# Three gate products moved from beside the chunked scan to between the convolution's tiles

## The chip, the cores and the metric

The kernel runs on one core of one Trainium2 chip. The metric is the device time of one execution in microseconds (us). Three runs of the kernel before gave 1928.44, 1927.75 and 1927.33 us; the median is 1927.75.

Short names: TensorE is PE (matrix products), VectorE is DVE (elementwise), ScalarE is ACT (elementwise, and copies out of PSUM), GpSimd is POOL, SyncE is SP (it issues most DMAs). Each runs its own instructions in order.

## What is computed

One encoder layer on 512 tokens of width 1024, in float32:

```
proj = rmsnorm(x) @ w_in                  -> u_s5, z, xbc, dt_raw, gate_a, gate_b
y_a  = glu(gelu(s5_bidirectional(u_s5)))               # the state-space branch (S5)
xbc  = silu(conv5(xbc) + b)  -> xs (8 tiles), B (2), C (2)
y_b  = ssd_bidirectional(z, xs, B, C, dt) @ w_out      # the chunked scan (SSD)
h    = x + (sigmoid(gate_a)*y_a + sigmoid(gate_b)*y_b) @ w_o
h    = h + peer_ffn(rmsnorm(h));  out = rmsnorm(h)
```

A tile is 128 of the output columns of a projection, for all 512 tokens. `gate_b` has eight tiles (gb0 to gb7), and so have `z`, `gate_a` and the convolution's `xs` (x0 to x7). The order in which the tiles are made is free as long as each is there when it is read. gate_b is read only after both branches are done.

## The kernel before, in words

**One stream of products.** `stream_T` (L159) takes a list of jobs, one per tile. A job loads 512 KB of weights through SP (L140), rounds them on ACT to `w_hi` (L143), subtracts to get `w_lo` on DVE or POOL (L144), and makes 8 x 3 matmuls of 512 columns (L151 to L153), then calls the tile's own evacuation. The load, the rounding and the subtraction of a job are issued one job ahead (L172). There are three buffers for raw weights, two each for `w_hi` and `w_lo`, and two PSUM tiles `mm`. The subtraction of gate_b's weights is on DVE (P_GB, L26), those of z and gate_a on POOL (P_REST, L25), those of the x tiles on POOL but for x3 and x7, which are on DVE (P_IN, L24). The first twelve jobs (N_RAW) use unsplit float32 matmuls instead (L176).

**Evacuations.** A gate_b tile: one tanh on ACT and a store to DRAM issued by ACT (`ev_gb`, L730). A z tile: a tanh on ACT, a multiply on DVE, a store (`ev_z`, L722). An x tile goes through `conv` (L459): two copies on ACT (L466, L469), four multiply-adds on DVE (L471), a tanh on ACT (L472) and a last DVE instruction that writes `xcT` (L473). `cvraw` and `cvacc` have two buffers each, so tile n is evacuated only when tile n-2 has gone through L473.

**Two stages, each a weave.** `weave` (L66) takes the next step of whichever of two generators has the smaller share done. In the first stage it weaves the first N_IN = 22 jobs, weight W_IN = 30, with the 96 steps of the S5 branch, weight 160. In the second it weaves the other 35 jobs, weight W_REST = 65, with the 60 steps of the SSD scan, weight 120: `ssd_prep` (4 steps, L533) transposes the x and B tiles, and `ssd_group` (4 groups of 14 steps, L557) makes the states (L585, L594), the product of C and B (L604), four rounds of decay matrices (L633 to L643) and products (L619, L621), and the group's norm (L663 to L683).

The program order that comes out is also a priority: when the program is built, a planner gives each engine, in turn, the earliest instruction of the program that it holds to be ready, so an engine's queue can run ahead of the program order, and is fixed before the kernel runs.

The job order (L737 to L752) is

```
        easy = gate_b + rest
        work = jobs[:4] + easy[:EASY] + jobs[4:] + easy[EASY:]
        for f in range(8):
            work += [gate_a[f], glu[8 + f], glu[f]]
```

where `jobs` holds four u tiles, the B and C tiles, dt and x0 to x7, and `rest` the z tiles. With EASY = 4 the first stage runs u0-u3, gb0-gb3, B, B, C, C, dt, x0 to x7, gb4. The second runs gb5, gb6, gb7, z0 to z7, and then eight times a gate_a product and two products of the gated linear unit (`glu`, four row blocks each, so 12 matmuls).

**After both.** `merge` (L836) splits the scan's result into `yh` and `yl` (L845, L156, L157), multiplies by `w_so` (first product of `yh` and `yl`), reads gate_b back from DRAM, and multiplies by `w_o`. Everything later waits for this.

Of the kernel before, what the change touches and what calls it, by code (L numbers as in the profile page):

```python
# [36 lines left out]
X_POOL = 0  # L37
EASY = 4
E_ACT = (1,)
N_IN = 22  # L40
N_RAW = 12
LAST = 2
R_ORDER = (0, 1, 2, 3)
YY_LATE = True
PR_S5 = 0
W_IN = 30
W_REST = 65
PR_SSD = 0
MAGIC = 12582912.0
# [16 lines left out]
def weave(*fibers):  # L66

    live = [[g, 0, float(n)] for g, n in fibers]
    while live:
        live.sort(key=lambda f: f[1] / f[2])  # L70
        f = live[0]
        try:
            next(f[0])
            f[1] += 1
        except StopIteration:
            live.remove(f)


def ahead(tc, gen, offset):

    while True:
        with tc.high_priority(offset):
            try:
                next(gen)
            except StopIteration:
                return
        yield


class Kernel:  # L90
# [596 lines left out]
    def front(self):  # L687
# [27 lines left out]
        def ev_u(q):  # L715
            def f(ps):
                t = self.cvp.tile([128, 8, 64], F32, name="ust", bufs=2)
                nc.scalar.copy(t, ps.rearrange("p (j t) -> p t j", t=8))
                nc.scalar.dma_start(self.u_d[q], t.rearrange("p t j -> p (t j)"))
            return f  # L720
# [17 lines left out]
        jobs = [(win[q], 128, ev_u(q)) for q in range(4)]  # L738
# [3 lines left out]
        jobs = self.jobs(jobs, 8, xh, xl, P_IN)  # L742
# [4 lines left out]
        glu = self.jobs([(I["w_glu"][f], 128, e(f % 8)) for e, a in ((self.ev_gu, 0), (self.ev_gs, 8))  # L747
                         for f in range(a, a + 8)], 4, self.yah, sl(self.yal), P_GLU)
        easy = gate_b + rest
        work = jobs[:4] + easy[:EASY] + jobs[4:] + easy[EASY:]  # L750
        for f in range(8):
            work += [gate_a[f], glu[8 + f], glu[f]]  # L752

# [16 lines left out]
        def s5():  # L770
            self.s5_prep()
            for _ in range(S5_SKIP):
                yield
            late = None
            for q in range(8):
                p, d = self.s5_params(q), self.s5_data(q)
                for _ in range(S5_A):
                    next(p)
                    yield
                if late:  # L780
                    for _ in late:
                        yield
                for _ in p:
                    yield
                for _ in range(S5_B):
                    next(d)
                    yield
                late = d
            for _ in late:
                yield  # L790

        with tc.tile_pool(name="cvp", bufs=1, reuse_waits="tile") as self.cvp, tc.tile_pool(name="s5c", bufs=1, reuse_waits="tile") as self.s5c, \
                tc.tile_pool(name="s5p", bufs=1, reuse_waits="tile") as self.s5p:
            weave((islice(stream, N_IN), W_IN), (ahead(tc, s5(), PR_S5) if PR_S5 else s5(), 160))
        self.dbg("xcT", self.xcT.rearrange("p a b -> p (a b)"))
# [518 lines left out]
```

## Time and profile before

| what | value |
|---|---|
| median of three runs | 1927.75 us |
| the profiled execution's own time | 1927.67 us |
| its span, first to last instruction | 1925.9 us |
| mean granted TensorE clock | 0.974 of full speed |
| busy share of the span: PE, DVE, ACT, POOL | 94%, 76%, 43%, 36% |
| S5 stage, about | 0 to 247 us |
| SSD stage, about | 247 to 468 us |
| the rest (merge, routing, expert products) | 468 us to the end |

Busy time is counted per engine. PE being busy does not mean that it runs at its peak: matmuls overlap, so the start-to-start time of two neighbours is what one costs. The granted clock says at what share of 2.4 GHz TensorE ran.

### The profile page before, as it was taken

To read this page: it belongs to the slowest core of one execution; us is meant where nothing else is said; L and a number is where in the kernel's file an instruction comes from. 1 tells how busy PE (TensorE), PEld (TensorE's weight loads), DVE (VectorE), ACT (ScalarE), POOL (GpSimd) and SP (SyncE) were. 2 spreads that over 40 slices of the span, in tenths; PEclk is the share of its full clock that TensorE was granted. 3 is DMA by queue.
4 is the path that set the end of the run, shared out by engine and by line. 5 is a ranking of instruction groups with operands and counts; after the bars stand their busy time and mean duration, and the time that the engine had idled before them with its cause. 6 is when DMAs were issued, how large, how long until landed. Compare 5 with 4: busy or idle time off the path is not lost.

```text
span 1925.9 us, 27091 instructions
## 1 busy us (share of the span) xinstructions
PE 1815.1 (94%) x9351; PEld 1553.0 (81%) x9351; DVE 1466.3 (76%) x3280; ACT 828.4 (43%) x1422; POOL 697.7 (36%) x583
## 2 busy tenths in 40 slices
PE   7999799999989988787898999999999999999998
PEld 3557677677878877777898999999999999999886
DVE  6999956686547799989848877777777777776676
ACT  4235355555333337686842333333333333333333
POOL 1112014444023355554534443434434343343341
PEclk9999899999999989889899999999999999999999
DMA  4322255444432233333499989898888888986665
GB/s 151 98 84 66 70 177 170 147 159 158 165 134 99 86 122 137 147 143 126 181 303 321 383 305 313 277 315 307 296 295 313 308 282 309 312 283 231 235 255 199
DMA packets 174825, 407.45 MB, mean 212 GB/s; under 512 B 20000, under 2 KB 77088, under 8 KB 171616
## 3 DMA queue, kind: packets, MB, share of 16 engines
q1 hardware_dynamic: 129472, 258.27, 39.9%
q0 software_dynamic: 36864, 134.23, 19.7%
q10 hardware_dynamic: 8352, 13.21, 2.0%
q8 instruction: 74, 1.21, 0.3%
q14 instruction: 63, 0.52, 0.1%
HBM read 367.28 MB, written 37.32 MB: 210 GB/s over the span
## 4 chain that ended last, share of the span: by engine, by line
PE 60%; DVE 11%; DMA 3%; ACT 2%; issue 1%; POOL 1%; DVEq 0%; POOLq 0%; SPq 0%; ACTq 0%
PE acc L1097 9%; PE acc L1098 9%; PE acc L1096 9%; PE hid L153 7%; PE hid L151 7%; PE hid L152 7%; PE mm L151 3%; PE mm L153 3%; PE mm L152 3%; PE sm L1042 3%; DMA G<-G_d 2%; DVE oh L1023 2%; DVE oh L1024 1%; DVE ohm L957 1%; PE sm L903 1%
## 5 line engine op out<-in xcount | busy, mean ns | idle before, releaser
L143 ACT CAST w_hi<-w_raw 128x1024 fp32r<-128x1024 f32 (+2 forms) x197 | 199.2, 1012 | 446.6 <-PE hid L152 213.3
L153 PE MATMUL hid<-x2h,w_lo 128*128 128x384 f32 x1024 | 358.3, 350 | 15.1 <-POOL w_lo L144 9.6
L151 PE MATMUL hid<-x2h,w_hi 128*128 128x384 f32 x1024 | 356.0, 348 | 9.6 <-ACT w_hi L143 9.6
L152 PE MATMUL hid<-x2l,w_hi 128*128 128x384 f32 x1024 | 355.3, 347 | 0.0
L144 POOL TENSOR_TENSOR w_lo<-w_raw,w_hi 128x1024 fp32r<-128x1024 f32 (+1 forms) x88 | 204.0, 2320 | 364.2 <-ACT w_hi L143 361.4
L1098 PE MATMUL acc<-vh,Wl 128*128 128x512 f32 x768 | 301.0, 392 | 0.0
L1097 PE MATMUL acc<-vl,Wh 128*128 128x512 f32 x768 | 300.7, 392 | 0.0
L1096 PE MATMUL acc<-vh,Wh 128*128 128x512 f32 x768 | 298.8, 389 | 0.0
L1113 POOL DMA_INDIRECT rowg<-in_u_dram,idx x128 | 195.0, 1523 | 276.3 <-DVE rowg L1125 190.9
L144 DVE TENSOR_TENSOR w_lo<-w_raw,w_hi 128x1024 fp32r<-128x1024 f32 (+1 forms) x109 | 132.7, 1217 | 173.2 <-ACT w_hi L143 173.2
L1113 POOL DMA_INDIRECT rowg<-in_v_dram,idx x128 | 165.4, 1292 | 273.4 <-DVE acc L1135 210.2
L153 PEld LDWEIGHTS hid<-x2h,w_lo 128*128 128x128 f32 x1024 | 198.0, 193 | 17.3 <-POOL w_lo L144 11.5
L151 PEld LDWEIGHTS hid<-x2h,w_hi 128*128 128x128 f32 x1024 | 198.0, 193 | 14.3 <-ACT w_hi L143 10.5
L156 ACT CAST Wh<-F 128x384 fp32r<-128x384 f32 x128 | 65.8, 515 | 317.9 <-PE acc L1097 276.0
L152 PEld LDWEIGHTS hid<-x2l,w_hi 128*128 128x128 f32 x1024 | 197.6, 193 | 3.7
L1098 PEld LDWEIGHTS acc<-vh,Wl 128*128 128x128 f32 x768 | 144.2, 188 | 30.4 <-DVE Wl L157 0.2
L157 DVE TENSOR_TENSOR vl<-v_raw,vh 128x1024 fp32r<-128x1024 f32 x128 | 156.4, 1222 | 15.3 <-ACT vh L156 14.4
L1096 PEld LDWEIGHTS acc<-vh,Wh 128*128 128x128 f32 x768 | 144.3, 188 | 28.1 <-ACT vh L156 0.4
L1097 PEld LDWEIGHTS acc<-vl,Wh 128*128 128x128 f32 x768 | 144.2, 188 | 28.1
L1135 DVE SCALAR_TENSOR_TENSOR acc<-rowg,act,acc 128x1024 f32<-128x1024 f32 x127 | 162.5, 1279 | 2.7 <-DMA rowg<-in_v_dram,idx 2.6
L1125 DVE SCALAR_TENSOR_TENSOR rowg<-rowg,xn 128x1024 f32<-128x1024 f32 x128 | 151.8, 1220 | 1.2 <-DMA rowg<-in_u_dram,idx 1.2
L1042 PE MATMUL sm<-oh,oh 128*128 128x128 f32 x768 | 131.8, 298 | 12.2 <-DVE oh L1024 12.1
(395 smaller groups left out, 3403.9 us busy)
## 6 DMA issues: line engine op xcount, KB each, us to landing
w_raw<-in_ut_dram SPq DMA_DIRECT2D x128, 512.0 KB
v_raw<-in_v_dram SPq DMA_DIRECT2D x128, 512.0 KB
G_d<-stg SPq DMA_DIRECT2D x24, 1024.0 KB
G<-G_d SPq DMA_DIRECT2D x16, 1536.0 KB
w_raw<-in_w_in_dram SPq DMA_DIRECT2D x40, 512.0 KB
RB<-rows_d SPq DMA_DIRECT2D x32, 256.0 KB
w_raw<-in_w_q_dram SPq DMA_DIRECT2D x16, 512.0 KB
E<-rows_d SPq DMA_DIRECT2D x32, 128.0 KB
```

Source lines behind the costliest of these rows:

```text
L143: nc.scalar.copy(hi, raw)
L144: (lo_eng or nc.vector).tensor_sub(lo, raw, hi.bitcast(F32))
L151: mm(ps, ahi(k), bhi(k), start=start and k == 0, stop=False)
L152: mm(ps, ahi(k), blo(k), start=False, stop=False)
L153: mm(ps, alo(k), bhi(k), start=False, stop=stop and k == nk - 1)
L157: (lo_eng or self.nc.vector).tensor_sub(lo, src, hi.bitcast(F32))
L1042: T.matmul(ps[:, j * 128:(j + 1) * 128], o2, o1, start=True, stop=True)
L1096: mm(a, wh[:, ts], vh[:, hs], start=k == 0, stop=False)
L1097: mm(a, wh[:, ts], vl[:, hs], start=False, stop=False)
L1098: mm(a, wl[:, ts], vh[:, hs], start=False, stop=k == 127)
L1113: nc.gpsimd.indirect_dma_start(out=r, out_offset=None, in_=tab, in_offset=bass.IndirectOffsetOnAxis(ap=self.idx0[:, k:k + 1], axis=0))
L1135: d = V.scalar_tensor_tensor(self.acc0, r, act[:, k:k + 1], self.acc0, op0=OP.mult, op1=OP.add)
```

## The change

gb5, gb6 and gb7 move into the first stage, and gb4 to gb7 now stand each behind a pair of x tiles. The first stage has 25 jobs and the second 32. W_IN goes up with N_IN; W_REST stays.

```
-N_IN = 22
+N_IN = 25
...
-W_IN = 30
+W_IN = 34
...
-        work = jobs[:4] + easy[:EASY] + jobs[4:] + easy[EASY:]
+        work = jobs[:4] + easy[:EASY] + jobs[4:9]
+        for f in range(4):
+            work += jobs[9 + 2 * f:11 + 2 * f] + easy[EASY + f:EASY + f + 1]
+        work += easy[EASY + 4:]
```

The first stage's order is now u0-u3, gb0-gb3, B, B, C, C, dt, x0, x1, gb4, x2, x3, gb5, x4, x5, gb6, x6, x7, gb7; the second begins with z0.

## Rows read from the trace of the kernel before

**Rows 1.** Busy us (instructions) of each engine by stretch, granted clock, DMA.

```profile
core 0: us, PE busy (x) PEld busy (x) DVE busy (x) ACT busy (x) POOL busy (x), PEclk, DMA share, GB/s
18.00:166.00 148.00, 144.60 (x682) 86.37 (x680) 137.81 (x377) 56.41 (x109) 21.26 (x45) 1.00 0.30 91
166.00:247.00 81.00, 66.81 (x422) 54.84 (x423) 73.06 (x141) 36.54 (x67) 10.31 (x25) 0.92 0.30 82
```

**Rows 2.** Timeline of PE, two neighbours inside a product (start, duration).

```profile
154.26 0.39 PE L151 MATMUL mm<-xh,w_hi 128*128 128x512 f32 x1
154.49 0.39 PE L152 MATMUL mm<-ring,w_hi 128*128 128x512 f32 x1
```

**Rows 3.** Whom PE waited for, 140 to 257 us: total, times, longest.

```profile
PE mm L153 <- DVE w_lo L144: 5.0, 1, 5.0
PE sm L511 <- DVE adt L507: 4.4, 1, 4.4
```

**Rows 4.** Timelines of ACT, DVE and POOL: weights of x6 (POOL) and x7 (DVE).

```profile
198.78 2.37 POOL L144 TENSOR_TENSOR w_lo<-w_raw,w_hi 128x1024 fp32r<-128x1024 f32 x1 [5.45 <-ACT w_hi L143]
...
212.98 1.06 ACT L143 CAST w_hi<-w_raw 128x1024 fp32r<-128x1024 f32 x1 [2.33 <-PE mm L152]
...
233.80 1.22 DVE L144 TENSOR_TENSOR w_lo<-w_raw,w_hi 128x1024 fp32r<-128x1024 f32 x1
```

**Rows 5.** Timelines: x2's last matmuls and evacuation; x7's evacuation and last DVE instruction.

```profile
172.20 0.63 PE L152 MATMUL mm<-ring,w_hi 128*128 128x512 f32 x1
...
186.59 0.59 ACT L466 COPY cvraw<-mm 128x512 f32<-128x512 f32 x1
...
247.60 0.57 ACT L466 COPY cvraw<-mm 128x512 f32<-128x512 f32 x1
...
256.36 0.69 DVE L473 SCALAR_TENSOR_TENSOR xcT<-cvraw,cvacc 128x512 f32<-128x512 f32 x1 [0.31 <-ACT cvraw L472]
```

**Rows 6.** Timeline of PE: last products of groups 0 and 1, next group's C-B product.

```profile
314.62 0.44 PE L621 MATMUL yy<-E,S 128*64 128x128 f32 x4
...
341.00 1.16 PE L604 MATMUL sm<-xcT 64*128 64x128 f32 x8
...
362.62 0.44 PE L621 MATMUL yy<-E,S 128*64 128x128 f32 x4
...
383.97 1.16 PE L604 MATMUL sm<-xcT 64*128 64x128 f32 x8
```

**Rows 7.** Timelines of PE and DVE, from the scan's last product to w_so's first.

```profile
449.87 0.44 PE L621 MATMUL yy<-E,S 128*64 128x128 f32 x4
...
458.25 1.41 DVE L683 SCALAR_TENSOR_TENSOR yb<-yb,nwh,sm 128x512 f32<-128x512 f32 x2 [2.43 <-PE sm L678]
459.58 4.90 DVE L157 TENSOR_TENSOR yl<-yb,yh 128x512 fp32r<-128x512 f32 x8
465.46 1.24 DVE L144 TENSOR_TENSOR w_lo<-w_raw,w_hi 128x1024 fp32r<-128x1024 f32 x1 [0.98 <-ACT w_hi L143]
468.07 0.39 PE L151 MATMUL mm<-yh,w_hi 128*128 128x512 f32 x1
```

**Rows 8.** Timeline of PE: matmuls behind the wait of 5.02 us, and later ones.

```profile
235.80 0.69 PE L441 MATMUL sm<-toe,U 128*64 128x128 f32 x2
...
238.41 0.39 PE L441 MATMUL sm<-toe,U 128*64 128x128 f32 x2
...
239.51 0.38 PE L443 MATMUL sm<-x0n,spimv 128*64 128x128 f32 x2
```

**Rows 9.** Timelines of POOL and DVE: a subtraction on POOL, one DVE line beside and alone.

```profile
150.66 2.84 POOL L144 TENSOR_TENSOR w_lo<-w_raw,w_hi 128x1024 fp32r<-128x1024 f32 x1 [3.61 <-ACT w_hi L143]
151.25 2.81 DVE L254 TENSOR_TENSOR mpr<-mpr,s5tmp 128x512 f32<-128x512 f32 x1
...
181.83 0.67 DVE L254 TENSOR_TENSOR mpr<-mpr,s5tmp 128x512 f32<-128x512 f32 x1
```

## The prediction

> **What bounds the kernel now.** I read the busy time by stretch first. From 18 to 166 us PE is busy 144.60 of 148 us and DVE 137.81: nothing can be put beside that for nothing. From 166 to 247 us, the second half of the S5 stage, DVE is busy 73.06 of 81 us and PE only 66.81, at a granted clock of 0.92 [rows 1]. So PE has 81 - 66.81 = 14.2 us of waiting there, and 0.08 x 81 = 6.5 us more are lost to the clock: about 20.7 us in which other products could stand. The view of waits says for whom: 5.0 us for one subtraction of weights on DVE, 4.4 us for the dt path on DVE [rows 3]. DVE is the limit of that stretch, and PE stands in line for it.
>
> After 247 us PE is nearly always busy. Its timeline there is scan products with stream products between them and short waits. The stage ends when the last stream product is through: the scan's result is finished at 458.25 + 1.41 us, yet the first w_so product starts at 468.07 [rows 7], because PE is still working off the stream. A stream product taken out of that stage is worth its PE time, as long as PE has other work in its place at the end.
>
> **What the change moves.** A split product is 24 matmuls, and neighbours start 154.49 - 154.26 = 0.23 us apart [rows 2], so a gate product costs PE 24 x 0.23 = 5.5 us and a glu product (12) 2.8. Three gate products, 16.5 us of PE, go from the SSD stage to the S5 stage. No work is added or dropped in all, so the kernel gains what PE waits less in the first stage and loses what it waits more in the second.
>
> **Part one, the S5 stage: +7.0 us.** Before x7's last matmul stand gb4, gb5 and gb6 that were not there: 16.5 us. (gb7 and z0 then stand where gb4 and gb5 stand now, behind x7, 11.0 us each way: 0.) The scan needs x7, so whatever of the 16.5 us isn't hidden delays everything after it.
> - gb4 stands behind x1, ahead of x2. Today x2's last three matmuls run around 172.20 us and its tile is picked up at 186.59 [rows 5], since ACT and DVE are behind. Pushing x2 back by 5.5 us leaves 8 us to spare: 0. If that cover were gone it would cost 5.5.
> - gb5 stands behind x3. PE's waits other than the two long ones are 14.2 - 5.0 - 4.4 = 4.8 us [rows 1, 3]; I count 4.0 of them as filled, and 1.5 of its 5.5 us as delay.
> - gb6 stands ahead of x6. Its weights are subtracted on DVE and issued late in the program, as x7's are today: x7's were rounded at 212.98 and subtracted only at 233.80, whereas x6's were subtracted on POOL 20 us earlier in the same line [rows 4]. So gb6 takes the place that x7 has now, with its 5.0 us wait, and x6 or x7 follows it: 5.5 in full.
> - DVE: a gate's subtraction is 1.22 us (x7's row is the same shape [rows 4]). Ahead of x7's end three stand there today (gb4, gb5, gb6 issued ahead), four afterwards: +1.2 us, beside PE's lateness: 0, and at worst 3 x 1.22 = 3.7 if all three are late work on DVE.
> - Queues: three more 512 KB loads pass SP ahead of the S5 loads and three tanh with their stores pass ACT. ACT is busy 36.54 of 81 us [rows 1]: 0.
> - W_IN: 22/30 = 0.733 and 25/34 = 0.735, so the weave keeps its pace; u to dt come some 8 of the 96 S5 steps earlier relative to the branch. Up to 166 us both engines are full either way: I take 0.
>
> Bounds of this part: 0 (20.7 us of room exceed 16.5) and 16.5 (nothing hidden). I take 7.0, nearer to the low end, because room is there and the two products that are due early can use it.
>
> **Part two, inside the scan: -5.0 us.** W_REST stays 65, so each later job comes three places earlier beside the scan, and since the tail of the list repeats in threes (gate_a, glu, glu), groups 1 to 3 see the very pattern they see now. Only the gap between group 0's last product and group 1's C-B product changes: it holds z6, z7 and a gate_a now (16.5 us), and afterwards what the gap between groups 1 and 2 holds now, a gate_a and two glu (11.0). The first gap lasts 341.00 - 314.62 = 26.4 us, the second 383.97 - 362.62 = 21.4 [rows 6]. So 5.0 of the 5.5 us are gained.
>
> **Part three, the end of the scan: -6.3 us.** Behind the scan's last product there now stand glu, gate_a, glu, glu in program order, 13.9 us; afterwards one glu, 2.8. Then the scan's own chain sets the end. From the last product at 449.87 to its last multiply at 458.25 and the first `yl` at 459.58 + 0.69 (one of eight in 4.90 us, with their overlap) it is 460.3 - 449.9 = 10.4 us, against 468.07 - 449.87 = 18.2 now [rows 7]: 7.8 gained. PE then waits twice within this chain, some 4 us in all. Behind the wait of 5.02 us six groups took 238.41 - 235.80 = 2.6 us, where five took 1.1 at full clock a moment later [rows 8]: 1.2 GHz for a while, 1.3 us lost, 1.5 with the first matmul. I take those 1.5 off. Lower bound of the gain: the subtraction for the first w_so product, which stands behind all eight `yl` in DVE's order today (465.46 + 1.24 = 466.7, [rows 7]), stays there: 468.07 - 466.7 = 1.4.
>
> **The sum.** +7.0 - 5.0 - 6.3 = -4.3 us. The profiled execution took 1927.67 us (span 1925.9 and 1.8 around it), the same within 0.1 us as the median: 1927.7 - 4.3 = 1923.4 us. Everything behind 468 us is unchanged and only starts earlier.
>
> One row bears on what stands beside x7. While POOL subtracts weights (2.84 us) one DVE instruction takes 2.81 us that takes 0.67 alone [rows 9]. z0 and z1 are subtracted on POOL; they come up beside x7's convolution, where gb4 and gb5 on DVE stand now. The Trainium skill, "SBUF — State Buffer", section "Who interferes with whom", says that a DVE instruction with two SBUF inputs and a GpSimd instruction that reads SBUF exclude each other for a whole instruction. The row agrees; by that rule the last rival below is due.
>
> **The rivals.**
> - *Hidden whole.* The 20.7 us take in all three gates; x7 ends as now: -5.0 - 6.3 = -11.3, 1916.4 us. For it: the size of the room. Against it: the order of each queue is fixed beforehand, so a wait for DVE is filled only if the planner saw it coming.
> - *DVE's late subtractions stop the stream (slower).* gb4, gb5 and gb6 each wait for a 1.22 us subtraction behind some 20 us of older DVE work, as x7 does [rows 4]; with two weight buffers nothing overtakes for long, and x7 goes back by all 16.5 us: +16.5 - 11.3 = +5.2, 1932.9 us. It decides once x7 is later by more than 11.3 us. For it: DVE is busy 90% of that stretch [rows 1]. Against it: gb4 and gb5 are issued earlier than x7.
> - *The end gives nothing.* The w_so subtraction stays behind the `yl`: +7.0 - 5.0 - 1.4 = +0.6, 1928.3 us. For it: today's order. Against it: that w_so's weight buffers come free earlier once the glu products are done.
> - *POOL against x7's convolution.* From pick-up to last result x7 now takes 256.36 + 0.69 - 247.60 = 9.5 us [rows 5], and 11.0 us of products cover it. Two POOL subtractions add 2 x (2.81 - 0.67) = 4.3: 13.8 against 11.0, 2.8 us uncovered: 1926.2 us.
>
> **How the numbers follow.** Forecast 0.40, hidden whole 0.16, stopped stream 0.24, no gain at the end 0.14, POOL 0.06. 0.2% is 3.9 us, about what a measurement of this kernel can tell from no change. Of the forecast's 0.40 I give 0.29 to more than 3.9 us gained, the rest to less: faster 0.16 + 0.29 = 0.45; within 0.2% 0.11 + 0.14 + 0.06 = 0.31; slower 0.24. The forecast's own range is 1919 to 1926, from part one between 3 and 10 us. The range reaches to the first rival's time and to the second's, 1915.5 to 1933.0, leaving out what lies beyond each.
>
> **What would show it.** Right: x7's pick-up (247.60 now) near 254.5 us; PE's waits of 166 to 247 us down from 14.2 to under 8; the gap behind group 0 near 21 us; w_so's first product about 10 us behind the scan's last, with two waits and a clock below 1 there; that product at about 463.8 instead of 468.07. Wrong: x7 within 2 us of now, or beyond 260; new long waits of PE for `w_lo` from DVE; w_so's first product still 15 us or more behind the scan's last; a difference that arises after w_so.

## The result, and the profile after

The changed kernel took 1939.01 us in the median (six runs, 1937.14 to 1941.90) against 1927.95 us for the kernel before beside it (six runs, 1923.94 to 1928.80): a ratio of 1.0067, 95% interval 1.0053 to 1.0082. It is 11.1 us slower, where 4.3 us less were forecast, and lies above the range. The profiled execution took 1941.9 us, its span 1939.8 against 1925.9.

The first view, busy time by stretch of the changed kernel, answers to [rows 1]; the columns are the same:

```profile
18.00:166.00 148.00, 137.98 (x611) 81.33 (x610) 134.65 (x369) 55.01 (x105) 14.85 (x41) 0.97 0.30 90
166.00:247.00 81.00, 72.01 (x465) 57.45 (x463) 64.60 (x130) 35.25 (x67) 12.49 (x27) 0.92 0.22 64
```

In the second stretch PE is busier by 5.2 us, as the forecast wanted. But in the first it is busy 6.6 us less than before (137.98 against 144.60), and DVE does 8.5 us less work from 166 to 247 us. The S5 branch, which gives DVE its work, has fallen behind: its last transpose on PE starts at 256.88 us instead of 241.17. Whom PE waited for, 140 to 270 us, the changed kernel (to be held against [rows 3]):

```profile
PE mm L151 <- ACT cvraw L466: 5.7, 2, 4.2
PE sm L361 <- DVE x0r L347: 3.7, 3, 1.9
PE mm L153 <- POOL w_lo L144: 3.2, 2, 1.9
...
PE mm L153 <- DVE w_lo L144: 0.9, 1, 0.9
```

The 5.0 us for a subtraction on DVE are gone; in their place stand many waits, for the evacuation of x tiles and for the branch's own DVE steps. No single one explains the loss.

Timelines of ACT, DVE and PE of the changed kernel: x7's pick-up and last DVE instruction [rows 5], then the end of the scan [rows 7]:

```profile
271.10 0.57 ACT L466 COPY cvraw<-mm 128x512 f32<-128x512 f32 x1
281.35 0.68 DVE L473 SCALAR_TENSOR_TENSOR xcT<-cvraw,cvacc 128x512 f32<-128x512 f32 x1
...
472.03 2.27 DVE L144 TENSOR_TENSOR w_lo<-w_raw,w_hi 128x1024 fp32r<-128x1024 f32 x1 [0.24 <-ACT w_hi L143]
473.98 0.44 PE L621 MATMUL yy<-E,S 128*64 128x128 f32 x4
477.22 0.39 PE L151 MATMUL mm<-yh,w_hi 128*128 128x512 f32 x1
483.12 1.41 DVE L683 SCALAR_TENSOR_TENSOR yb<-yb,nwh,sm 128x512 f32<-128x512 f32 x2 [3.30 <-PE sm L678]
484.44 4.90 DVE L157 TENSOR_TENSOR yl<-yb,yh 128x512 fp32r<-128x512 f32 x8
485.19 0.79 PE L152 MATMUL mm<-yl,w_hi 128*128 128x512 f32 x1 [2.18 <-DVE yl L157]
```

x7 is picked up at 271.10 us instead of 247.60: 23.5 us late, twice what parts two and three (11.3 us) could pay for. The end of the scan went as forecast: the subtraction for w_so (472.03) now stands ahead of the `yl`, and PE waits for the scan's own chain. From the last product to w_so's second matmul it is 485.19 - 473.98 = 11.2 us, where 10.4 were expected and [rows 7] show 18.2.

Timelines of PE: the scan's first C-B product in the kernel before, then in the changed kernel, and there the last products of groups 0 and 1 and the next group's C-B product [rows 6]:

```profile
281.46 1.16 PE L604 MATMUL sm<-xcT 64*128 64x128 f32 x8
...
308.69 1.16 PE L604 MATMUL sm<-xcT 64*128 64x128 f32 x8
...
341.85 0.44 PE L621 MATMUL yy<-E,S 128*64 128x128 f32 x4
...
364.18 1.16 PE L604 MATMUL sm<-xcT 64*128 64x128 f32 x8
...
386.67 0.44 PE L621 MATMUL yy<-E,S 128*64 128x128 f32 x4
...
406.43 1.16 PE L604 MATMUL sm<-xcT 64*128 64x128 f32 x8
```

The first gap is 22.3 us (26.4 before, 21.4 expected), the second 19.8 (21.4 before). That is what part two wanted, but it was lost ahead of the scan, at a place where the forecast had 0: from x7's pick-up to the first C-B product it is 308.69 - 271.10 = 37.6 us, and 281.46 - 247.60 = 33.9 before. From x7's pick-up to the scan's last product nothing was gained (202.9 us, 202.3 before); only the end of the scan gave something back.

By stages, profile against profile: x7's pick-up +23.5 us; first C-B product +27.2; the scan's last product +24.1; w_so's third matmul +17.3 (485.78, 468.5 before); w_o's first +19.9, for w_so ran at 1.2 GHz up to 490.9 us, behind the waits of the scan's end (granted clock 0.50 from 485.8 to 490.9 us, 0.93 over its 46 us, 1.00 before); the end of the span +13.9. Of the 6 us that come back between w_o and the end, 4.5 are the shorter time of a later stage at a higher clock, shown under the last heading; no edit reached that stage.

### The profile page after: what moved, and what is told of

Read it like the earlier page. It is cut to its first block, busy times and chain, and to the rows that moved or that the text cites. A ratio compares the mean times of both kernels' runs of the same rounds, so it can differ in the third digit from the quotient of the medians.

```text
span 1939.8 us, 27081 instructions
## 1 busy us (share of the span) xinstructions
PE 1819.8 (94%) x9351; PEld 1551.8 (80%) x9351; DVE 1468.9 (76%) x3280; ACT 828.3 (43%) x1422; POOL 696.8 (36%) x583
## 4 chain that ended last, share of the span: by engine, by line
PE 62%; DVE 11%; DMA 3%; ACT 1%; issue 1%; POOL 1%; DVEq 0%; POOLq 0%; SPq 0%; ACTq 0%
PE acc L1100 9%; PE acc L1101 9%; PE acc L1099 9%; PE hid L153 7%; PE hid L151 7%; PE hid L152 7%; PE mm L151 3%; PE mm L152 3%; PE mm L153 3%; PE sm L1045 3%; DMA G<-G_d 2%; DVE oh L1026 2%; DVE oh L1027 1%; DVE ohm L960 1%; PE sm L906 1%
## 5 line engine op out<-in xcount | busy, mean ns | idle before, releaser
L1116 POOL DMA_INDIRECT rowg<-in_v_dram,idx x128 | 169.7, 1326 | 271.9 <-DVE acc L1138 208.0
L151 PEld LDWEIGHTS hid<-x2h,w_hi 128*128 128x128 f32 x1024 | 197.3, 193 | 14.1 <-ACT w_hi L143 10.4
```

Of the source, the lines that this page charges most:

```text
L151: mm(ps, ahi(k), bhi(k), start=start and k == 0, stop=False)
L1116: nc.gpsimd.indirect_dma_start(out=r, out_offset=None, in_=tab, in_offset=bass.IndirectOffsetOnAxis(ap=self.idx0[:, k:k + 1], axis=0))
```

## The experiments

Fifteen kernels. Each median stands beside that of the kernel before on the same chip, which was 1925.7 to 1927.9 us. The theories, by the numbers that the expectations use, were: the larger W_IN, costed at nothing, moves early products ahead of the branch (1, the pace); the gates between the x tiles are not hidden (2, the places); DVE's late subtractions stop the stream (3).

**The two halves of the change.** `pace30` is the changed kernel with the old W_IN, `before_pace34` the kernel before with the new one (the second diff).

```
-W_IN = 34
+W_IN = 30
```

```
-W_IN = 30
+W_IN = 34
```

> The changed kernel with W_IN back at 30, the order of the jobs and N_IN = 25 as changed. Theory 1 (pace: the higher weight puts the early products ahead of the S5 branch in program order, and the branch ends 15.7 us later for it): the branch's last transpose goes back from 256.9 to 241-247 us, x7's pick-up from 271.1 to 250-258, the time to 1922-1931 us. Theory 2 (places: the gate products between the x tiles hold up the stream and the branch whatever the weight): last transpose still beyond 252, time 1935-1942. Theory 3 (the gates' subtractions on DVE come late and stop the stream): as theory 2, 1935-1942.

> The kernel before with W_IN = 34 alone; no gate product moves. Theory 1 (pace): the branch's last transpose goes from 241.2 to 250-257 us and the time to 1934-1942 us. Theories 2 and 3 (the gates' places or subtractions): last transpose 239-244, time 1926-1930, no change.

`pace30`: 1933.06 us, ratio 1.0029 (1.0009 to 1.0049). `before_pace34`: 1942.63 us, 1.0086 (1.0069 to 1.0102). The pace alone, with no gate moved, costs 16 us; the gates alone 6.5. Neither theory holds alone: in `pace30` the branch's last transpose is back at 238.80 us, as theory 1 had it, but x7's pick-up is not. Timeline of ACT, `pace30`:

```profile
264.38 0.57 ACT L466 COPY cvraw<-mm 128x512 f32<-128x512 f32 x1
```

The two costs don't add up to the 11.1 us of the whole change; that x7 and the branch can be late side by side is my reading of it. What the pace does is seen in PE's timeline. The kernel before: start of the branch's fifth block, dt's transpose, the decay product behind dt, the branch's last transpose:

```profile
127.18 0.38 PE L361 MATMUL sm<-x0r,bm 128*32 128x128 f32 x2 [0.19 <-DVE x0r L347]
...
151.27 0.43 PE L483 MATMUL sm<-ident,dtraw 32*128 32x32 f32 x4
...
170.35 0.77 PE L511 MATMUL sm<-adt,mask_f 128*128 128x128 f32 x2 [4.37 <-DVE adt L507]
...
241.17 0.71 PE L451 MATMUL sm<-ident,yg 64*128 64x64 f32 x8
```

The same with W_IN = 34 (`before_pace34`):

```profile
140.21 0.43 PE L483 MATMUL sm<-ident,dtraw 32*128 32x32 f32 x4 [1.19 <-ACT dtraw L480]
...
160.23 0.77 PE L511 MATMUL sm<-adt,mask_f 128*128 128x128 f32 x2 [4.27 <-DVE adt L507]
163.35 0.41 PE L361 MATMUL sm<-x0r,bm 128*32 128x128 f32 x2
...
260.57 0.71 PE L451 MATMUL sm<-ident,yg 64*128 64x64 f32 x8
```

The fifth block starts at 163.35 instead of 127.18: dt, x0, x1, x2 and the 4.3 us wait for dt's chain have gone ahead of it. Four of the branch's eight blocks are then left behind that point instead of three, and the last transpose is 19.4 us later. PE didn't stay full: from 166 to 247 us it is busy 61.96 us, 66.81 before. What it waited for is one step of the branch on DVE. From 166 us to the branch's end, first in the kernel before, then in `before_pace34`:

```profile
PE sm L361 <- DVE x0r L347: 0.5, 1, 0.5
...
PE sm L361 <- DVE x0r L347: 14.2, 3, 8.9
```

The products that stood beside the branch's late blocks had been used up early: from 214 to 246 us PE started 5 matmuls of the stream, 47 in the kernel before. x6 had been picked up at 222.33 us, and x7's weights were subtracted on DVE no earlier than 237.95.

**Other paces.** The kernel before with 32, in `before_pace32`, and with 26, in `before_pace26`.

```
-W_IN = 30
+W_IN = 32
```

```
-W_IN = 30
+W_IN = 26
```

> The kernel before with W_IN = 32. Theory 1b (the pace costs in proportion, as each raw product that comes ahead of a block of the branch pushes it by some 7 us): the branch's last transpose 247-256, time 1932-1938. Theory 1a in its weaker form (what counts is whether dt comes ahead of block 4; at 32 it stands behind block 4's first products): last transpose 240-246, time 1925-1931.

> The kernel before with W_IN = 26: the branch comes earlier against the products, dt behind block 5. Theory 1a (dt's place): dt is behind block 4 already at 30, so the branch gains at most one block: last transpose 225-242, but x3 to x7 are then behind the branch in program order, time 1922-1935. Theory 1b (the pace is a trade of branch against products that 30 balances): branch 10-20 us earlier, x7's pick-up as much later, time 1930-1942.

32 gave 1935.25 us, 1.0049 (1.0029 to 1.0069), a little over half the loss; 26 gave 1931.59, 1.0027 (0.9994 to 1.0061), too scattered to call. So the loss grows from 30 upwards, and nothing is shown to be gained below it. `before_pace32` also shows that a late branch reaches the scan by another way than x7. Timelines of ACT and PE, `before_pace32`: x7's pick-up, the branch's last transpose, the scan's first C-B product:

```profile
247.56 0.59 ACT L466 COPY cvraw<-mm 128x512 f32<-128x512 f32 x1
255.31 0.71 PE L451 MATMUL sm<-ident,yg 64*128 64x64 f32 x8
...
291.74 1.16 PE L604 MATMUL sm<-xcT 64*128 64x128 f32 x8
```

x7 is on time (247.60 before), yet the scan starts 10.3 us later. SP issued the scan's first row loads (L567) at 254.78 us, 240.03 before: about as much later as the branch's end. What ties them to it (the program order, or memory that the branch still held) no run separates.

**Is it dt alone?** dt goes behind x1: `before_pace34_dt` does it in `before_pace34`, `after_dt` in the changed kernel.

```
-        work = jobs[:4] + easy[:EASY] + jobs[4:] + easy[EASY:]
+        work = jobs[:4] + easy[:EASY] + jobs[4:8] + jobs[9:11] + jobs[8:9] + jobs[11:] + easy[EASY:]
```

```
-        work = jobs[:4] + easy[:EASY] + jobs[4:9]
-        for f in range(4):
+        work = jobs[:4] + easy[:EASY] + jobs[4:8] + jobs[9:11] + jobs[8:9] + easy[EASY:EASY + 1]
+        for f in range(1, 4):
```

> The kernel before with W_IN = 34 and dt two places later, behind x1, so that in program order it stands behind the branch's block 4 again, as at W_IN = 30. Theory 1a (the harm of the pace is dt's place: at 34 it comes ahead of block 4, and that block's products wait on PE behind the dt path): block 4's first product goes from 163 back to 127-140 us, the branch's last transpose from 261 to 240-250, the time from 1942.6 to 1925-1933. Theory 1b (the pace itself: all products ahead of the branch cost it PE and DVE time): last transpose stays beyond 253, time 1936-1944.

> The changed kernel with dt two places later, behind x1. Theory 1a: the branch's last transpose goes from 257 to 240-250, x7's pick-up from 271 to 258-266 (the gates still cost their PE time), the time to 1927-1934, as with W_IN = 30. Theory 1b: last transpose beyond 253, time within 3 us of the changed kernel, 1936-1942.

`before_pace34_dt`: 1938.09 us, 1.0060 (1.0041 to 1.0079); `after_dt`: 1933.07, 1.0024 (1.0008 to 1.0040). In the first the fifth block is back at 143.08 us, yet the last transpose stays at 260.85: dt's place alone isn't what holds the branch up. In the changed kernel it helps by about 6 us (last transpose 251.15 instead of 256.88, x7's pick-up 259.88). Theory 1 held, but not in its narrow form (1a, dt's place).

**The early part of the stream or the late one?** The stream's count starts at 1.6 jobs, so that the early jobs stand as late against the branch as at W_IN = 30, while the x tiles stand closer together.

```
-def weave(*fibers):
+def weave(*fibers, head=0.0):
...
+    live[0][1] = head
...
-            weave((islice(stream, N_IN), W_IN), (ahead(tc, s5(), PR_S5) if PR_S5 else s5(), 160))
+            weave((islice(stream, N_IN), W_IN), (ahead(tc, s5(), PR_S5) if PR_S5 else s5(), 160), head=1.6)
```

`before_pace34_head` does so in `before_pace34`, `after_head` in the changed kernel.

> The kernel before with W_IN = 34, and the stream's count starts at 1.6 jobs, so that its jobs come 1.6 jobs later against the branch; the raw products and dt stand about where they stand at W_IN = 30, the x tiles a little ahead of it. Without the late start W_IN = 34 gave 1942.6 us, with the branch's fifth block beginning at 163 us and its last transpose at 261.1. Theory A (the raw products and dt, ahead of the branch's blocks, push the branch back): fifth block back to 127 to 135 us, last transpose 239 to 247, time 1925 to 1932. Theory B (the x tiles, closer together in the branch's second half): last transpose still 252 or later, time 1938 to 1944.

> The changed kernel with the same late start. Without it 1939.0 us, the branch's last transpose at 257.4 and x7's pick-up at 271.1. Theory A: last transpose 239 to 247, pick-up 258 to 266, time 1928 to 1935, as the changed kernel gave with W_IN = 30 (1933.1). Theory B: last transpose 252 or later, pick-up 268 or later, time 1936 to 1942.

`before_pace34_head`: 1925.78 us, 0.9997 (0.9980 to 1.0014). The whole 16 us are back. PE's timeline of `before_pace34_head`, with one line more in the program, so L362 is L361 of before and so on:

```profile
129.04 0.38 PE L362 MATMUL sm<-x0r,bm 128*32 128x128 f32 x2 [0.28 <-DVE x0r L348]
...
152.73 0.43 PE L484 MATMUL sm<-ident,dtraw 32*128 32x32 f32 x4
...
247.04 0.71 PE L452 MATMUL sm<-ident,yg 64*128 64x64 f32 x8
```

The block stands ahead of dt again. So the price of the larger W_IN lies in the early part of the stream. `after_head` fell between the theories: 1939.77 us, 1.0059 (1.0036 to 1.0082). The branch ends at 243.98 us as theory A wanted, 12.9 us earlier than in the changed kernel, but x7 is picked up at 267.69, only 3.4 earlier. With the branch on time x7 is still late, as it is in `pace30`, which has the gates without the pace. w_so starts 5.9 us earlier than in the changed kernel's profile; the median shows none of it. In the profiles 4.9 us of it are lost again in the later stage, by its clock (below); the rest is open.

**Where the gates stand.** `gates_behind` is the changed kernel with the order of before (the gates all behind x7, 25 jobs, W_IN = 34), `gates_behind30` the kernel before with 25 jobs at W_IN = 30.

```
-        work = jobs[:4] + easy[:EASY] + jobs[4:9]
-        for f in range(4):
-            work += jobs[9 + 2 * f:11 + 2 * f] + easy[EASY + f:EASY + f + 1]
-        work += easy[EASY + 4:]
+        work = jobs[:4] + easy[:EASY] + jobs[4:] + easy[EASY:]
```

```
-N_IN = 22
+N_IN = 25
```

> N_IN = 25 and W_IN = 34 as changed, but gb4 to gb7 stand behind x7, as gb4 does in the kernel before. Theory 1 (pace): the branch is as late as in the changed kernel (250-257), time 1932-1941. Theory 2 (places): x7's pick-up near 248 and the gates behind it, time 1924-1930. Theory 3 (DVE subtractions): these stand behind the branch and hold up nothing, time 1924-1930.

> N_IN = 25 alone: the order and W_IN = 30 as before, so that gb4 to gb7 stand behind x7. Theory 1 (pace) with the terms of the prediction: branch as before, x7's pick-up 246-250, the scan's first C-B product 5 to 12 us later than 281.5 (two more gates than before stand behind x7, and only the convolution's time covers them), the end of the scan gives 11 us back: 1922-1930. Theory 2 (the gates' places between the x tiles are what costs at 30): the same, 1922-1930, against 1933 with the gates between the tiles. If it is 1931 or more, moving three gates into the first stage costs wherever they stand.

`gates_behind`: 1944.50 us, 1.0094 (1.0077 to 1.0111). `gates_behind30`: 1929.25, 1.0009 (0.9991 to 1.0027). At W_IN = 34 the gates are better off between the x tiles (1939.0); at 30 no better than behind them (1933.1), where the time is not shown to differ from the kernel before. Timeline of PE, first C-B product of the scan, in `gates_behind30`:

```profile
297.37 1.16 PE L604 MATMUL sm<-xcT 64*128 64x128 f32 x8
```

and in `pace30`:

```profile
299.93 1.16 PE L604 MATMUL sm<-xcT 64*128 64x128 f32 x8
```

Against 281.46 in the kernel before, three more jobs behind x7 put the scan off by 15.9 us, nearly their full PE time (16.5), and three gates between the x tiles by 18.5. Between the tiles nothing was hidden, taking the three together.

**One gate, two gates.** In the kernel before, at W_IN = 30, gb4 alone goes behind x1 (`one_gate`); then gb5 also behind x3 (`two_gates`).

```
-        work = jobs[:4] + easy[:EASY] + jobs[4:] + easy[EASY:]
+        work = jobs[:4] + easy[:EASY] + jobs[4:11] + easy[EASY:EASY + 1] + jobs[11:] + easy[EASY + 1:]
```

```
-N_IN = 22
+N_IN = 23
...
-        work = jobs[:4] + easy[:EASY] + jobs[4:] + easy[EASY:]
+        work = jobs[:4] + easy[:EASY] + jobs[4:11] + easy[EASY:EASY + 1] + jobs[11:13] + easy[EASY + 1:EASY + 2] + jobs[13:] + easy[EASY + 2:]
```

> The kernel before with gb4 alone moved, from behind x7 to behind x1 (N_IN = 22, W_IN = 30, nothing else). As predicted (gb4 there is hidden, 0 us): x7's pick-up 246-249.5 us as before, time 1924-1929. Nothing hidden (what the run with all four gates between the tiles at W_IN = 30 shows: 16.8 us for three): x7's pick-up 252-255, and since gb4 no longer stands behind x7 the scan starts 0 to 3 us later: 1926-1932.

> The kernel before at W_IN = 30 with gb4 behind x1 and gb5 behind x3 (23 jobs in the first stage), gb6, gb7 and the rest as before. With gb4 alone moved x7's pick-up was 248.4 us and the time 1925.9; with three it was 264.4 and 1933.1. The prediction's price for gb5, 1.5 us: pick-up 248 to 251, time 1922 to 1928. If each gate after the first costs its whole 5.5 us of PE: pick-up 253 to 257, time 1926 to 1931. If most of the three gates' 16.8 us hangs on the second: pick-up 258 or later, time 1930 or more.

`one_gate`: 1925.91 us, 0.9985 (0.9969 to 1.0001). `two_gates`: 1947.23, 1.0112 (1.0092 to 1.0133). ACT's pick-ups of x4 and x7, and PE's first C-B product, in `one_gate`:

```profile
224.54 0.59 ACT L466 COPY cvraw<-mm 128x512 f32<-128x512 f32 x1 [0.49 <-PE mm L153]
...
248.41 0.59 ACT L466 COPY cvraw<-mm 128x512 f32<-128x512 f32 x1 [1.48 <-PE mm L153]
...
282.27 1.16 PE L604 MATMUL sm<-xcT 64*128 64x128 f32 x8
```

and the pick-ups of gb5, x4 and x7 in `two_gates`:

```profile
229.59 0.58 ACT L733 ACTIVATE ost<-mm 128x512 f32<-128x512 f32 x1
...
240.09 0.57 ACT L466 COPY cvraw<-mm 128x512 f32<-128x512 f32 x1
...
259.66 0.58 ACT L466 COPY cvraw<-mm 128x512 f32<-128x512 f32 x1
```

gb4 costs x7 0.8 us: hidden, as predicted. It gains nothing either: though it no longer stands behind x7, the scan starts 0.8 us later too, and the time is that of the kernel before. gb5 costs x7 another 11.3 us, not 1.5. It is picked up near where x4 was (229.59 against 224.54), x4 comes 15.6 us later, and x5 to x7 come behind the branch's end (240.24 us). Busy time from 166 to 247 us in `one_gate`:

```profile
166.00:247.00 81.00, 72.00 (x449) 58.85 (x450) 72.65 (x143) 37.51 (x68) 11.77 (x25) 0.92 0.33 92
```

in `two_gates`:

```profile
166.00:247.00 81.00, 67.89 (x437) 54.95 (x438) 67.84 (x136) 34.99 (x64) 12.29 (x22) 0.94 0.31 89
```

and in `pace30`, with all three:

```profile
166.00:247.00 81.00, 72.24 (x443) 58.40 (x444) 66.41 (x136) 35.09 (x66) 8.86 (x20) 0.89 0.36 99
```

Busy time times clock (an estimate of work at full speed) is 61.5 us before [rows 1], 66.2 with one gate, 63.8 with two, 64.3 with three. By that estimate the first gate put 4.7 us of its 5.5 into the room, and the other two added none. In `pace30` x7 came another 4.7 us after that of `two_gates`, for gb6.

That `two_gates` is slower than `pace30`, with one gate fewer, is a matter of the second stage: x7 is 12.1 us late there and w_so's first product (489.77 us) 21.7. Busy time of the scan's stretch, from C-B product to w_so, in the kernel before:

```profile
281.50:468.00 186.50, 177.53 (x974) 136.59 (x973) 135.08 (x246) 99.95 (x245) 85.20 (x50) 0.97 0.46 148
```

and in `two_gates`:

```profile
293.20:489.80 196.60, 180.37 (x951) 139.60 (x950) 134.05 (x242) 98.45 (x244) 82.04 (x49) 0.91 0.45 137
```

Whom PE waited for there, in `two_gates` (the same two waits were at most 1.4 and 1.2 us long in the kernel before):

```profile
PE yy L619 <- POOL E L643: 7.2, 3, 4.0
PE sm L671 <- ACT sq L666: 6.5, 3, 4.5
```

Waits of 4 to 4.5 us appear, and the granted clock over the stretch falls from 0.97 to 0.91, some 12 us of 200 (an estimate, 0.06 of the stretch). The list of products taken up there repeats in threes, and a shift by one instead of three puts other products into the scan's gaps: that this is the cause fits, but no run shifts the list alone.

**The subtractions on POOL.** gb4 to gb7 get their subtractions on POOL, in the changed kernel (`gates_pool`) and in `pace30` (`pace30_pool`).

```
-P_GB = (0,)
+P_GB = (0, 0, 0, 0, 1, 1, 1, 1)
```

> The changed kernel with the weights of gb4 to gb7 subtracted on POOL, not on DVE. Theory 3 (late DVE subtractions): x7's pick-up 255 us or earlier, time 1922-1931. Theories 1 and 2: the branch's last transpose stays beyond 252, time within 3 us of the changed kernel, 1936-1943.

> The changed order with W_IN = 30 and the weights of gb4 to gb7 subtracted on POOL. Theory 3 (at this pace the gates wait for DVE: gb4's weights were rounded at 157 and subtracted at 172): x7's pick-up goes from 264.4 to 250-259 us, time 1922-1930. Rival (the gates cost their PE and buffer time wherever they are subtracted, and POOL's 2.4 us block DVE): x7's pick-up 262-272, time 1932-1942.

`gates_pool`: 1949.32 us, 1.0127 (1.0110 to 1.0143), slower than any of the three theories had it. `pace30_pool`: 1935.56, 1.0041 (1.0022 to 1.0060). Without DVE's subtractions it is slower or no better. These two runs alone don't settle it, for POOL's subtractions have a price of their own: in `pace30_pool` the branch's last transpose is at 252.22 us instead of 238.80. But in `pace30` the view of PE's waits from 140 to 270 us names no `w_lo` of DVE at all, and in the changed kernel 0.9 us: PE doesn't stand in line for these subtractions, and theory 3 falls.

**More filler at the scan's end.** `pace30` with W_REST = 59, so that more products are left behind the scan.

```
-W_REST = 65
+W_REST = 59
```

> The changed order with W_IN = 30 and W_REST = 59, so that three products stand behind the scan's last product again instead of one. If the end of the scan is as the prediction has it (products there fill waits of some 4 us): the gap from the scan's last product to w_so goes from 10.7 back to 13-18 us, the scan itself is 4-8 us shorter, no slow clock in w_so, time 1927-1934, 0 to 4 us below the run with 65. If the fill has no worth: within 1.5 us of 1933 and the same clock.

1937.60 us, 1.0062 (1.0040 to 1.0084), 4.5 us more than `pace30`. The gap ahead of w_so grew from 10.7 to 19.2 us and the scan's last product came no earlier (463.5 against 462.8 us): my expectation of a gain missed. No kernel run here is shown to beat the one before; `one_gate` comes nearest.

## Why the prediction was wrong, point by point

- **The sum.** Expected -4.3 us, measured +11.1 (the profiles differ by 13.9). Two terms of part one failed and made x7 23.5 us late instead of 7.0: 16.5 us amiss. In the changed kernel parts two and three also fell short: 3.6 us had come back by w_o, 11.3 were expected. Against that stand the 6 us behind w_o that no term had, most of them a later stage's clock; without them the miss would be larger.
- **W_IN: "Up to 166 us both engines are full either way: I take 0."** This failed. The prediction had the fact, some 8 of the branch's 96 steps, and drew the wrong conclusion. With the gates in place the pace costs some 5 us (11.1 - 6.5, each against the kernel before beside it), without them 16. Engines that are full now have no idle time to lose, but they have an order. The new order put the branch's late blocks where fewer products stood beside them, PE waited 14.2 us for DVE there (`before_pace34`), and the scan's start followed the branch's end.
- **The gates: +7.0.** At the old pace x7's pick-up moved by 264.4 - 247.6 = 16.8 us, the term's upper bound. gb4's 0 was right (0.8). gb5's 1.5, and so the 7.0, was mis-sized: gb5 alone cost 11.3. I counted PE's waits as room. What the runs showed is that one product fits: by busy time and clock 66.2 us of work in the stretch with gb4, no more with the others (63.8, 64.3). That the rest of the waits lie among branch steps that each wait for DVE, where a further product only moves the tiles, is my reading of it.
- **Part two, -5.0.** The gap behind group 0 shrank by 4.1 us in the changed kernel: right for the gap. From the first C-B product to the scan's last product the changed kernel gained 3.1 us, `pace30` 5.8. But the 0 for what stands between x7 and that first product was wrong: +3.7 us in the changed kernel, +1.7 in `pace30`.
- **Part three, -6.3.** In `pace30` the way from the scan's last product to w_so shrank by 7.8 us and w_so at its lower clock took 1.9 more: -5.9. Right (in the changed kernel 7.0 and 2.6, so -4.4), and the rival that the end gives nothing falls. Parts two and three together: 16.8 us at x7 had become 5.0 at w_so in `pace30`, and 6.9 at w_o, so 9.9 came back where 11.3 were predicted.
- **The slower rival** had +16.5 for x7 and 1932.9 us; `pace30` shows 16.8 and 1933.06. That its price came true was luck, for its mechanism was wrong: PE's wait for DVE's `w_lo` went away instead of growing, and taking the subtractions off DVE did not help.
- **POOL against x7's convolution** came about too, at 1.5 us instead of 4.3: from pick-up to last result x7 takes 281.35 + 0.68 - 271.10 = 10.9 us, 9.5 before. Timelines of POOL and DVE, changed kernel:

```profile
270.36 4.32 DVE L471 SCALAR_TENSOR_TENSOR cvacc<-cvraw,cvw,cvacc 128x512 f32<-128x512 f32 x3
271.28 2.85 POOL L144 TENSOR_TENSOR w_lo<-w_raw,w_hi 128x1024 fp32r<-128x1024 f32 x1 [14.88 <-ACT w_hi L143]
...
278.38 0.74 DVE L471 SCALAR_TENSOR_TENSOR cvacc<-cvraw,cvw,cvacc 128x512 f32<-128x512 f32 x1
278.70 2.64 POOL L144 TENSOR_TENSOR w_lo<-w_raw,w_hi 128x1024 fp32r<-128x1024 f32 x1 [4.58 <-DMA E<-rows_d]
279.05 2.38 DVE L635 TENSOR_SCALAR E<-RB,acs 128x128 f32<-128x128 f32 x1
```

Three multiply-adds of 0.74 us (each with two tensor inputs in SBUF) take 4.32 beside the first subtraction. The Trainium skill, "SBUF — State Buffer", section "Who interferes with whom", has a DVE instruction with two SBUF inputs and a GpSimd instruction that reads SBUF exclude each other; these rows agree with it. Beside the second subtraction it is another DVE instruction that is held, L635 of the scan, with one tensor input: 2.38 us, where the one before it took 0.27. x7's last one stands behind it in DVE's order and starts at 281.35, where the subtraction ends (278.70 + 2.64 = 281.34).

## What to carry to other kernels

Where two streams are woven into one program order, a weight that changes the order early is a change of its own: cost it by which chain's next step it moves back, also where all engines are full, and by what is then left to stand beside that chain later. Idle time of an engine, summed over a stretch, is not yet room for a product; try one moved product before three, since here the first was free (and gained nothing) and the second put the last tile back by twice its length. And where a list of filler repeats with a period, expect other gaps from a shift by part of a period.

## What the runs showed of the chip that I had not expected

A stage that no edit touched, the one-hot products of the routing, lasted 216.8 to 222.0 us, longer where the clock granted near its end was lower. Its last 56 us (52 in the changed kernel) in the kernel before:

```profile
905.00:961.00 56.00, 49.69 (x329) 47.57 (x327) 50.00 (x188) 50.31 (x99) 33.13 (x34) 0.89 0.42 161
```

and in the changed kernel:

```profile
924.00:976.00 52.00, 44.53 (x317) 41.88 (x316) 47.79 (x180) 47.97 (x93) 31.57 (x32) 0.97 0.45 173
```

Over all 17 profiles the stage took 220.0 to 222.0 us where the last 56 us ran at 0.89 to 0.91, and 216.8 to 218.2 where they ran at 0.94 or more, whatever was edited 700 us earlier. That is some 4 us either way, as much as the finer comparisons here rest on; the times at x7, the scan and w_so lie ahead of it. What sets it was not settled: there is one profile of each kernel, so it can't be said whether it belongs to the kernel or to the run.
